# A sliding-window copy on three DMA rings: another order of the rings' DMAs, one release of SyncE's list, 24 merged pairs

## The chip, the cores and the metric

The kernel runs on one core of one Trainium2 chip. The metric is the device time of one execution in microseconds (us), the median of several runs. The core has 16 DMA engines. DMAs are issued by three of its processors here: SyncE (SP), ScalarE (ACT) and GpSimd (POOL). Each has a ring of its own, whose packets all run on the same 16 engines. The profile shows SP's ring as q1, ACT's as q10 and POOL's, which software fills, as q0.

## What is computed

```python
def setup_inputs():
    batch, length, dim = (32, 4096, 256)
    window_size = 64
    stride = 32
    return {'x': np.random.randn(batch, length, dim).astype(np.float32), 'window_size': window_size, 'stride': stride}

def reference(x: np.ndarray, window_size: int, stride: int) -> np.ndarray:
    batch, length, dim = x.shape
    n_windows = (length - window_size) // stride + 1
    result = np.zeros((batch, n_windows, window_size, dim), dtype=np.float32)
    for i in range(n_windows):
        start = i * stride
        result[:, i] = x[:, start:start + window_size].copy()
    return result
```

It is a pure copy. A batch of x has 4096 rows of 1 KB. In blocks of 32 rows (32 KB) it has 128 blocks, and window w of its 127 windows is block w followed by block w + 1. So the output is 127 x 64 KB for each of 32 batches, 266 MB, and nearly every block is written twice: as the first half (half 0) of one window and as the second half (half 1) of the window before.

## The kernel before

No engine computes. The 32 batches are copied in two ways.

**Staged batches.** Twelve batches (the list `staged`, L151) go through the on-chip memory. `Staging.load` (L78) brings a batch into one of six tiles of 128 partitions by 32 KB, a block a partition: one DMA of 4 MB, or four of 1 MB for the first batch. `Staging.store` (L93) then writes all 128 blocks twice, once for each half, in one DMA of 4 MB or two of 2 MB a half. All of these are issued by ACT, in the order that `run` (L121) gives: six loads, six batches' stores, six loads, four batches' stores, and last `store_pair` (L102) for the last two batches. A load waits until the tile's former stores have landed, and a store until its load has. Since 128 blocks are written for 127 windows, each half's store also writes one block too many, into the batch beside it: half 0 of the next batch's window 0, or half 1 of the last window (126) of the batch before. `store_pair` first issues four stores, counted by the semaphore `spilt`, and one more, then waits for `spilt`, then issues the last three.

**Direct batches.** The other twenty (`direct`) are copied from x to the output in memory, by `Copier.windows` (L29): a DMA of n rows, each a half window (32 KB, when `half` is given) or a whole window (64 KB). Two rings share each direct batch but the last:

- SP's ring (`ring_d`) copies half windows, 16 rows (512 KB) a DMA, `blocks` (L166), from the list `halves` (L174): for each batch, windows 0, 16, 32, 63, 79, 95 and 111 as first window, and for each of them half 0 and then half 1. Pieces that a neighbour's staged store overwrites (`spoilt`, L175) are taken out and copied at the end of the list, each behind a wait for that neighbour's stores (L198 to L201). All of SP's DMAs add to `done`.
- POOL's ring (`ring_r`) copies windows 48 to 62, which SP leaves out, 15 whole windows (960 KB) a DMA, `remainder` (L170). `piece` is the longest run in elements: `DIRECT` lets a packet be 32 KB, `DIRECT // 2` halves it to 16 KB. The last batch's windows 48 to 62 come in parts, one DMA of 11 rows and four of 2 half rows, placed between the others (L183 to L187).

All engines read their instructions in order, so a wait holds back everything behind it on that engine. POOL issues its 24 DMAs without waiting. SP issues one DMA, waits until the software ring's DMA for `direct[7]` (`back[7]`) has landed, issues two, waits for `back[11]`, issues three, waits for `back[16]`, and then issues all the rest (L191 to L197), as fast as its ring takes them. The last thing on SP is a wait for every semaphore's total (L203).

Of the kernel before, what the change touches and what calls it, by code (L numbers as in the profile page):

```python
# [8 lines left out]
DIRECT, IN, OUT = 32768, 16384, 16384  # L9
# [124 lines left out]
@with_exitstack  # L134
def kernel(
    ctx: ExitStack,
    tc: tile.TileContext,
    x: bass.AP,
    window_size: bass.AP,
    stride: bass.AP,  # L140
    out: bass.AP,
):
    nc = tc.nc
    W, S = int(window_size), int(stride)
    B, L, D = x.shape
    n_win = (L - W) // S + 1
    assert out.shape == (B, n_win, W, D)
    c = Copier(x, out, B, L, D, W, S, n_win)


    staged = [1, 4, 7, 10, 13, 16, 19, 22, 24, 26, B - 3, B - 2]  # L151
    place = {b: g for g, b in enumerate(staged)}
    direct = [b for b in range(B) if b not in staged]
    pool = ctx.enter_context(tc.tile_pool(name="xb", bufs=1))
    st = Staging(c, tc, pool, x.dtype, staged, 6)
    ring_d, ring_s, ring_r = nc.sync, nc.scalar, nc.gpsimd
    done = tc.alloc_semaphore("done")
    rest = tc.alloc_semaphore("rest")
    back = {i: tc.alloc_semaphore(f"back{i}") for i in (7, 11, 16)}
    total = {done: 0, rest: 0, **dict.fromkeys(back.values(), 0)}  # L160

    def count(dma, sem):
        dma.then_inc(sem, 16)
        total[sem] += 16

    def blocks(part):  # L166
        for b, w, half in part:
            count(c.windows(ring_d, b, w, 16, half), done)

    def remainder(b, w, n, half=None, piece=DIRECT, sem=rest):  # L170
        count(c.windows(ring_r, b, w, n, half, piece), sem)

    first, last = 48, B - 1
    halves = [(b, w + (15 if w >= first else 0), half) for b in direct for w in range(0, 112, 16) for half in (0, 1)]  # L174
    spoilt = {(b + d, 0 if d > 0 else c.nw - 16, 0 if d > 0 else 1): g for b, g in place.items() for d in (1, -1) if b + d in direct}  # L175
    halves = [h for h in halves if h not in spoilt]
    spoilt = sorted(spoilt, key=spoilt.get)
    with tc.tile_critical():
        st.run(ring_s)

        pairs = iter([(first + d, half) for d in (0, 2) for half in (0, 1)])
        for i, b in enumerate(direct[:-1]):
            if i in (8, 9, 12, 13):  # L183
                w, half = next(pairs)
                remainder(last, w, 2, half, DIRECT // 2)
            if i == 3:
                remainder(last, first + 4, 11)  # L187
            remainder(b, first, 15, piece=DIRECT // 2 if i in (1, 2, 3, 13, 15, 18) else DIRECT, sem=back.get(i, rest))
        ring_r.drain()  # L189

        blocks(halves[:1])  # L191
        ring_d.wait_ge(back[7], 16)
        blocks(halves[1:3])
        ring_d.wait_ge(back[11], 16)
        blocks(halves[3:6])
        ring_d.wait_ge(back[16], 16)
        blocks(halves[6:])  # L197
        for h in spoilt:  # L198
            b = h[0] + (-1 if h[1] == 0 else 1)
            st.wait_stored(ring_d, place[b])  # L200
            blocks([h])  # L201
        total[st.ended] = st.count[st.ended]
        for sem, n in total.items():  # L203
            ring_d.wait_ge(sem, n)
# [35 lines left out]
```

## Time and profile before

| what | value |
|---|---|
| median of 3 runs | 748.66 us (748.11 to 748.69) |
| the profiled execution | 747.83 us |
| its span, first to last instruction | 746.1 us |
| bytes moved by DMA | 317.50 MB |
| read from memory, written to memory | 216.79 MB, 267.12 MB |
| SP's DMAs | 280 of 512 KB, median 84.0 us from issue to landing |
| ACT's DMAs | 15 loads, 38 stores |
| POOL's DMAs | 24 (19 of 960 KB, 1 of 704 KB, 4 of 64 KB) |
| busy time of POOL, the only engine that shows any | 13.9 us |

The span runs from the first instruction to the last. A DMA packet is one run of bytes on one DMA engine, data or the 4 bytes that count a semaphore; "from issue to landing" contains the time that a DMA stands in its ring. The DMA share is the mean busy share of the 16 engines in a slice or a window, and is up to a few per cent over 1 where a packet reaches into the next window. An SP or ACT instruction that issues a DMA also lasts as long as its ring is full.

### The profile page before, as it was taken

To read this page: it belongs to the slowest core of one execution; us is meant where nothing else is said; L and a number is where in the kernel's file an instruction comes from. 1 tells how busy PE (TensorE), PEld (TensorE's weight loads), DVE (VectorE), ACT (ScalarE), POOL (GpSimd) and SP (SyncE) were. 2 spreads that over 40 slices of the span, in tenths; PEclk is the share of its full clock that TensorE was granted. 3 is DMA by queue.
4 is the path that set the end of the run, shared out by engine and by line. 5 is a ranking of instruction groups with operands and counts; after the bars stand their busy time and mean duration, and the time that the engine had idled before them with its cause. 6 is when DMAs were issued, how large, how long until landed. Compare 5 with 4: busy or idle time off the path is not lost. (4 is left out here: it accounts for less than half of the span.)

```text
span 746.1 us, 414 instructions
## 1 busy us (share of the span) xinstructions
POOL 13.9 (2%) x28
## 2 busy tenths in 40 slices
POOL 7000000000000000000000000000000000000000
DMA  8999999999999999999999999999999999999998
GB/s 358 437 420 420 430 418 423 428 430 434 429 430 434 429 430 431 433 430 433 432 401 432 431 433 435 428 428 437 429 429 436 430 430 433 430 428 435 429 430 350
DMA packets 20370, 317.50 MB, mean 426 GB/s; under 512 B 5884, under 2 KB 5884, under 8 KB 5884
## 3 DMA queue, kind: packets, MB, share of 16 engines
q10 hardware_dynamic: 10064, 151.00, 47.6%
q1 hardware_dynamic: 8960, 146.82, 46.1%
q0 software_dynamic: 1344, 19.66, 6.2%
q14 instruction: 2, 0.02, 0.0%
HBM read 216.79 MB, written 267.12 MB: 649 GB/s over the span
## 5 line engine op out<-in xcount | busy, mean ns | idle before, releaser
L34 POOL DMA_DIRECT2D out_dram<-in_x_dram x24 | 13.7, 576 | 1.1 <-PEq L235 1.1
L221 POOL MEMSET const-float32-0.0<- 128x1 f32 x1 | 0.1, 98 | 0.2 <-issue 0.2
L221 POOL MEMSET const-bfloat16-1.0<- 128x1 bf16 x1 | 0.1, 101 | 0.0
L221 POOL MEMSET const-float32-1.0<- 128x1 f32 x1 | 0.1, 98 | 0.0
L221 POOL MEMSET const-uint8-127<- 128x1 uint8 x1 | 0.1, 98 | 0.0
## 6 DMA issues: line engine op xcount, KB each, us to landing
out_dram<-in_x_dram SPq DMA_DIRECT2D x280, 512.0 KB, 84.0
out_dram<-xb ACTq DMA_DIRECT2D x28, 2048.0 KB, 105.9
xb<-in_x_dram ACTq DMA_DIRECT2D x11, 4096.0 KB, 121.1
out_dram<-xb ACTq DMA_DIRECT2D x10, 4096.0 KB, 120.2
out_dram<-in_x_dram POOLq DMA_DIRECT2D x19, 960.0 KB, 51.7
xb<-in_x_dram ACTq DMA_DIRECT2D x4, 1024.0 KB, 15.3
out_dram<-in_x_dram POOLq DMA_DIRECT2D x1, 704.0 KB, 21.5
out_dram<-in_x_dram POOLq DMA_DIRECT2D x4, 64.0 KB, 54.1
```

The source lines that it names most:

```text
L34: return q.dma_start(out=self.oap((b * self.nw + w0) * 2 + h, [[2 * blk, n], row]), in_=self.xap(b * self.nb + w0 + h, [[blk, n], row]), m ...
L221: nc = _bacc.Bacc("TRN2", target_bir_lowering=False, num_devices=1)
```

## The change

Four things change, and the bytes copied do not.

- POOL's order: the four 2-row DMAs stand before indices 8, 9, 11 and 14 (before: 8, 9, 12, 13), the one of 11 rows before index 4 (before: 3), and the DMAs cut to 16 KB packets are 1, 3, 4, 6 and 15 (before: 1, 2, 3, 13, 15, 18).
- SP's waits: instead of three, there is one, behind the first DMA, for the last 15-row DMA of the software ring (index 18, the last of that ring). Everything else of SP's follows it.
- Merged pairs: for the 17 direct batches but the first two and the last, half 0 of windows 79 to 94 and 95 to 110 becomes one DMA of 32 rows (1 MB); for seven of them (b % 5 is 0 or 2) half 1 does too. SP then has 256 DMAs.
- Batches by halves: within a batch, `halves` has all of half 0 and then all of half 1.

```diff
-    back = {i: tc.alloc_semaphore(f"back{i}") for i in (7, 11, 16)}
-    total = {done: 0, rest: 0, **dict.fromkeys(back.values(), 0)}
+    back = tc.alloc_semaphore("back")
+    total = {done: 0, rest: 0, back: 0}
...
     def blocks(part):
-        for b, w, half in part:
-            count(c.windows(ring_d, b, w, 16, half), done)
-
-    def remainder(b, w, n, half=None, piece=DIRECT, sem=rest):
-        count(c.windows(ring_r, b, w, n, half, piece), sem)
+        for b, w, half, *n in part:
+            count(c.windows(ring_d, b, w, *(n or [16]), half), done)
+
+    def remainder(i, b, w, n, half=None, piece=DIRECT):
+        count(c.windows(ring_r, b, w, n, half, piece), back if i == len(direct) - 2 and n == 15 else rest)
 
     first, last = 48, B - 1
-    halves = [(b, w + (15 if w >= first else 0), half) for b in direct for w in range(0, 112, 16) for half in (0, 1)]
+    halves = [(b, w + (15 if w >= first else 0), half) for b in direct for half in (0, 1) for w in range(0, 112, 16)]
...
+    for b in direct[2:-1]:
+        halves[halves.index((b, 79, 0))] = (b, 79, 0, 32)
+        halves.remove((b, 95, 0))
+        if b % 5 in (0, 2):
+            halves[halves.index((b, 79, 1))] = (b, 79, 1, 32)
+            halves.remove((b, 95, 1))
...
-            if i in (8, 9, 12, 13):
+            if i in (8, 9, 11, 14):
                 w, half = next(pairs)
-                remainder(last, w, 2, half, DIRECT // 2)
-            if i == 3:
-                remainder(last, first + 4, 11)
-            remainder(b, first, 15, piece=DIRECT // 2 if i in (1, 2, 3, 13, 15, 18) else DIRECT, sem=back.get(i, rest))
+                remainder(i, last, w, 2, half, DIRECT // 2)
+            if i == 4:
+                remainder(i, last, first + 4, 11)
+            remainder(i, b, first, 15, piece=DIRECT // 2 if i in (1, 3, 4, 6, 15) else DIRECT)
         ring_r.drain()
 
         blocks(halves[:1])
-        ring_d.wait_ge(back[7], 16)
-        blocks(halves[1:3])
-        ring_d.wait_ge(back[11], 16)
-        blocks(halves[3:6])
-        ring_d.wait_ge(back[16], 16)
-        blocks(halves[6:])
+        ring_d.wait_ge(back, 16)
+        blocks(halves[1:])
```

## The prediction

> **What bounds the kernel now.** I read the page's parts 2 and 3 first: no compute engine works, so the only question is how busy the DMA engines are and how fast they move bytes while busy.
>
> ```profile
> DMA  8999999999999999999999999999999999999998
> GB/s 358 437 420 420 430 418 423 428 430 434 429 430 434 429 430 431 433 430 433 432 401 432 431 433 435 428 428 437 429 429 436 430 430 433 430 428 435 429 430 350
> DMA packets 20370, 317.50 MB, mean 426 GB/s; under 512 B 5884, under 2 KB 5884, under 8 KB 5884
> ...
> q10 hardware_dynamic: 10064, 151.00, 47.6%
> q1 hardware_dynamic: 8960, 146.82, 46.1%
> q0 software_dynamic: 1344, 19.66, 6.2%
> ```
>
> The 16 engines are busy from end to end: nothing on the chip waits for an idle DMA engine except at the two ends. q10 is ACT's ring (loads and stores of staged batches), q1 SP's ring (the direct copies), q0 POOL's software ring. Time can change only through bytes (317.50 MB, which the change leaves alone), through the rate, and at the ends. Next, the windows view, cut where the rate changes; its columns are window, length, POOL, clock, DMA share and GB/s.
>
> ```profile
> 0.00:10.00 10.00, 8.69 (x19) 1.00 0.77 300
> 10.00:45.00 35.00, 5.25 (x10) 1.00 1.01 430
> 45.00:98.00 53.00, 0.00 (x0) 1.00 1.00 424
> 98.00:120.00 22.00, 0.00 (x0) 1.00 1.00 413
> 120.00:365.00 245.00, 0.00 (x0) 1.00 1.01 431
> 365.00:390.00 25.00, 0.00 (x0) 1.00 1.00 410
> 390.00:702.00 312.00, 0.00 (x0) 1.00 1.01 431
> 702.00:740.00 38.00, 0.00 (x0) 1.00 1.01 430
> 740.00:746.00 6.00, 0.00 (x0) 1.00 0.43 183
> ```
>
> The steady rate is 431 GB/s, and it is reached whenever nothing disturbs. So the span is 317.50 MB / 431 GB/s = 736.7 us, plus what each window loses against 431: the start 10 x (431-300)/431 = 3.0; 10 to 98, 0.1 + 0.9 = 1.0; 98 to 120, 0.9; 365 to 390, 1.2; the end 0.1 + 3.5 = 3.6. Sum 746.4, against a span of 746.1. That execution took 747.83 (1.7 around the span), the median is 748.66, 0.83 more; I carry the difference that I find over to the median.
>
> Third, how the rings share an engine: the DMA view, for 120 to 365 and then for 45 to 98.
>
> ```profile
> q1 hardware_dynamic: 3368, 55.19, 52.5%
> q10 hardware_dynamic: 3368, 50.46, 48.1%
> ```
> ```profile
> q10 hardware_dynamic: 666, 10.34, 46.4%
> q0 software_dynamic: 670, 9.50, 42.1%
> q1 hardware_dynamic: 160, 2.62, 11.8%
> ```
>
> The packet counts of two rings that are both full are equal, 3368 to 3368 and 666 to 670: an engine takes one packet from each ring in turn, whatever its size. A packet may be 32 KB (1213 ns in the trace's packet records), 16 KB (611 ns) or the 4 bytes that count a semaphore (9 ns). A 16-row DMA of SP is, per engine, one 32 KB packet and one of 4 bytes, so two turns, and ACT moves 16 KB in each.
>
> Last, what SP and ACT wait for.
>
> ```profile
> SPq L34 <- DMA out_dram<-in_x_dram: 94.3, 3, 44.5
> SPq L34 <- DMA out_dram<-xb: 44.4, 2, 40.6
> SPq L204 <- DMA out_dram<-xb: 39.7, 1, 39.7
> ```
> ```profile
> 0.91 7.16 ACTq L43 DMA_DIRECT2D xb<-in_x_dram  x9
> ```
>
> SP's three waits for the software ring end at 46, 69 and 98.9 us in the trace. They cost nothing: ACT has queued nine loads (25 MB) by 8 us and POOL all 24 DMAs by 15 us, and the windows show the engines full meanwhile. The 40.6 us is SP's wait for the spilt stores before its last two DMAs; SP's ring holds about 17 DMAs then, which cover it.
>
> **The change, part by part.**
>
> *Merged pairs.* 24 DMAs go, 16 semaphore packets each: 384 packets, 24 an engine, by 9 ns = 0.2 us. Nothing hides it, since the engines are full; bounds 0 and 0.2, I take -0.2. Issue gets cheaper too, but SP issues behind a full ring and gains nothing. The merges also move turns: each takes one turn of SP's away in which ACT moved 16 KB, so SP's list gets ahead of ACT's by 24 turns.
>
> *Release by the last 15-row DMA.* Before, the software ring's last DMA lands at 110.7 us and SP has landed 8 DMAs by then. After, SP has 1. The software ring no longer shares with 7 x 0.524 = 3.7 MB, worth 8.7 us at 424 GB/s; one fewer of its DMAs is cut into 16 KB pieces (5, not 6), so 30 packets fewer, 2 turns an engine, in which ACT moves 0.5 MB or 1.2 us. It should land its last at about 110.7 - 8.7 - 1.2 = 101 us, and SP's list goes then, not at 98.9. SP's waiting is covered as before: ACT's first loads last to 132 us. Behind the wait stand all of SP's other DMAs, and nothing waits for those but the end. ACT, one packet for each of the software ring's, is where it was; SP is 7 DMAs, 14 turns, behind.
>
> *The two together at the end.* SP gains 24 turns and loses 14: its list ends 10 turns sooner against ACT's. Before, the rings ended within 1 us (743.3 and 744.2), SP last by about a turn. After, ACT has some 9 turns left alone: 9 x 16 engines x 16 KB = 2.4 MB, 5.5 us of the same work in another order. No window shows ACT alone. Bounds: at 431 GB/s it costs 0; at the 300 GB/s of the first 10 us, whose ramp makes it too dark, 2.4/0.300 - 5.5 = +2.5. I take 0, nearer the row of two rings with 16 KB packets (430 in 10 to 45). The spilt stores still end under SP's backlog, which shrinks from 17 DMAs by about 10 turns, 5 DMAs, to 12, so SP's last two again cost nothing.
>
> *Software ring's order, batches by halves.* Same bytes, no wait. Where a DMA of 15, 11 or 2 rows puts its rows, the page doesn't show. If each starts on the engine behind the last one's, the four pairs start on engines 3, 4, 3, 4 before and 3, 4, 4, 3 after: no engine's load changes; if not, an engine gets one 32 KB packet more or less, 1.2 us either way at most. I take 0. What can change is who touches memory near whom, and with it the slow stretches: 0.9 in 45 to 98, 0.9 in 98 to 120 (SP in batch 0), 1.2 in 365 to 390 (SP in batch 14 with w from 16 to 63, ACT ending batch 16's stores). The trace shows no cause for them. Bounds: all gone, -3.1; twice as much, +3.1. SP's five early DMAs no longer run as a third ring, and the windows with SP among three are slower (424, 413) than the two-ring one (430): I take a tenth of the whole, -0.3.
>
> In 100 to 120 the rate stays low after the software ring is empty (415 before 110, 413 after). The Trainium skill, HBM Reference, Specifications, gives some 716 GB/s for the memory that a pair of cores shares; three full rings would ask for up to 431 x 1.8 = 776 GB/s, read and written, and by that rule the 12 us of three rings go at 398, so that taking them apart gains 0.9. The row at 413 with two rings speaks against it as the cause; by the rule the sum would be 0.6 lower, still no measurable change.
>
> Sum: -0.2 + 0 + 0 - 0.3 = -0.5: 747.3 for the profiled execution, **748.2 us** for the median.
>
> **The rivals.**
>
> *A, the slow stretches dissolve (faster).* SP's new order puts batch 0 and batch 14 against other work of ACT's. For it: outside these stretches 600 us go at 431. Against: two of the three lie where SP or POOL merely copies as everywhere, so new meetings are as likely as old ones. Two thirds gone: -2.1 - 0.2 = 746.4.
>
> *B, the order by halves brings new slow stretches (slower).* Before, consecutive DMAs of SP write both halves of a window; after, seven or so in a row write the same half, 32 KB at a step of 64 KB, beside ACT's stores, which do the same. For it: the worst row (410) is one of SP copying beside ACT's stores of one half. Against: ACT's stores have this form for most of the run, at 431. One such stretch costs 0.9 to 1.2; it decides from two more on: 748.2 + 2.1 = 750.3, three give 751.3. Call it 750.7.
>
> *C, a ring alone is slow (slower).* ACT's 5.5 us alone at 300 GB/s: 748.2 + 2.5 = 750.7. From 1.7 dearer, some 330 GB/s, it shows. If the merges did not shift turns, SP would be left alone instead, with 14 turns, 7 DMAs or 3.7 MB, at the end; at 300 GB/s +3.7, 751.9. Against: equal packet counts in three windows.
>
> *D, the merge saves each DMA's fixed time.* SP's DMAs land one in 2.4 us while taking 84 us from issue to landing, so latency is hidden; if 2.4 us were a price by DMA and not by byte, 24 x 2.4 = 58 us would go: 690. The full engines exclude nearly all of it.
>
> **How the numbers follow.** About 0.2% (1.5 us) is what a measurement of this kernel can tell from no change. Forecast 0.50; A 0.26; B 0.15; C 0.08; D 0.01. Faster than 747.2: A and D, 0.27. Slower than 750.2: B and C, 0.23. The forecast's own range is 747.2 to 749.6; taking in the greater part of A and of B and C, 746.1 to 751.0.
>
> **What would show it.** Right: SP has one long wait that ends near 101 us; q1 has 8576 packets; the steady windows still give 431; SP's last data lands some 5 us before ACT's, and the last windows hold their rate. A shows as 45 to 120 and the stretch near batch 14 at 429 or more; B as windows under 425 after 120 us that were at 431; C as a low rate in the last 6 us before the end. I am wrong if SP ends last, if its wait ends far from 101, or if the time is outside the forecast's range with all windows at 431.

## The result and the profile after

The changed kernel took 751.07 us (median of 6 runs, 750.39 to 752.89), the kernel before 748.67 on the same chip (6 runs, 747.51 to 749.06): a ratio of 1.0035, interval 1.0025 to 1.0045. It is slower by 2.4 us, where 748.2 and no change was forecast. The profiled execution took 751.22, its span is 749.4, which is 3.3 more than before.

The page of the changed kernel, parts 2 and 3:

```profile
DMA  8999999999999999999999999999999999999998
GB/s 359 428 432 428 431 433 433 427 433 425 432 432 421 433 433 426 429 433 428 407 431 414 431 427 422 424 429 433 422 428 432 429 420 428 425 429 431 417 431 344
DMA packets 19954, 317.49 MB, mean 424 GB/s; under 512 B 5498, under 2 KB 5498, under 8 KB 5498
...
q10 hardware_dynamic: 10064, 151.00, 47.5%
q1 hardware_dynamic: 8576, 146.82, 46.1%
q0 software_dynamic: 1312, 19.66, 6.1%
```

The engines are as full as before and move the same bytes, with q1 down to the expected 8576 packets. What differs is the rate, from the tenth slice on: 421, 426, 414, 422 where the kernel before held about 430. The windows (start and end, length, POOL, clock, DMA share, GB/s), cut as in the prediction:

```profile
0.00:10.00 10.00, 8.70 (x19) 1.00 0.78 300
10.00:45.00 35.00, 5.25 (x10) 1.00 1.01 428
45.00:98.00 53.00, 0.00 (x0) 1.00 1.01 429
98.00:120.00 22.00, 0.00 (x0) 1.00 1.02 433
120.00:365.00 245.00, 0.00 (x0) 1.00 1.01 429
365.00:390.00 25.00, 0.00 (x0) 1.00 1.00 411
390.00:702.00 312.00, 0.00 (x0) 1.00 1.01 427
702.00:740.00 38.00, 0.00 (x0) 1.00 1.01 423
740.00:749.00 9.00, 0.00 (x0) 1.00 0.64 273
```

The same account as before: 317.49 MB / 431 GB/s = 736.6 us, plus the loss of each window: start 3.0; 10 to 120, 0.2 + 0.2 - 0.1 = 0.3 (before 1.9); 120 to 365, 1.1 (before 0); 365 to 390, 1.2 (1.2); 390 to 702, 2.9 (0); 702 to the end, 0.7 + 3.3 = 4.0 (3.6). Sum 749.1, against 749.4. So the change did win 1.6 us in the first 120, where the release and POOL's order act (no run has one without the other), and the steady part, which cost nothing before, gives 4.0 away.

SP's waits and, from 120 to 365, the turns:

```profile
SPq L34 <- DMA out_dram<-in_x_dram: 97.1, 1, 97.1
SPq L34 <- DMA out_dram<-xb: 51.4, 3, 41.1
```
```profile
q1 hardware_dynamic: 3283, 55.78, 53.3%
q10 hardware_dynamic: 3291, 49.43, 47.3%
```

One wait of SP's for the software ring is left and ends at 98.7 us in the trace, a little ahead of the 101 forecast. The rings still take turns packet by packet, 3283 to 3291, merges or not: with fewer 4-byte packets SP moves 55.78 MB in that window to ACT's 49.43, where it was 55.19 to 50.46.

In the trace's packet records the slow time is in data packets that last longer than their 611 ns (16 KB) or 1213 ns (32 KB). What they last beyond that, their surplus, sums to 3.8 us an engine over the steady part (130 to 350 and 410 to 695 us), where the kernel before has 0.4.

### The profile page after: what moved, and what is told of

Its sections match the earlier page's. It is cut to its first block, busy times and chain, and to the rows that moved or that the text cites. A ratio compares the mean times of both kernels' runs of the same rounds, so it can differ in the third digit from the quotient of the medians.

```text
span 749.4 us, 389 instructions
## 1 busy us (share of the span) xinstructions
POOL 13.9 (2%) x28
## 2 busy tenths in 40 slices
DMA packets 19954, 317.49 MB, mean 424 GB/s; under 512 B 5498, under 2 KB 5498, under 8 KB 5498
## 3 DMA queue, kind: packets, MB, share of 16 engines
q1 hardware_dynamic: 8576, 146.82, 46.1%
```

## The experiments

Each group of kernels ran on a chip of its own, with the kernel before timed beside it. That took 745.4 to 745.6 us on the first four groups' chips and 748.2 on the last one's; 748.7 had been measured at first. So only times of one group are compared.

**First group: each part taken out.** Three kernels undo or isolate a part; the fourth keeps the merges but deals the rows out in another way.

```diff
# no merge: the changed kernel without these lines
-    for b in direct[2:-1]:
-        halves[halves.index((b, 79, 0))] = (b, 79, 0, 32)
...
# merge alone: the kernel before with those lines and blocks() taking n
# no halves: the changed kernel
-    ... for b in direct for half in (0, 1) for w in range(0, 112, 16)]
+    ... for b in direct for w in range(0, 112, 16) for half in (0, 1)]
# rows apart: the changed kernel, for n == 32
+                out=self.oap((b * self.nw + w0) * 2 + h, [[2 * blk, 16], [32 * blk, 2], row]),
+                in_=self.xap(b * self.nb + w0 + h, [[blk, 16], [16 * blk, 2], row]),
```

> The changed kernel with all of SP's DMAs at 16 rows again (280 of them); the order by halves, the single release and POOL's order stay. Theory M (the merged DMAs stretch the packets around them): the windows from 120 to 700 us return to 431 GB/s outside batch 14, and the time is 748 to 749 if SP alone at the end is fast. SP lacks 14 turns without the merges, so it is left alone with some 7 DMAs (3.7 MB, about 8 us); if a ring of copies alone is slow this adds 1 to 4 us to the end and nowhere else. Theory H (the order by halves does it): windows from 200 to 700 stay at 427 to 428, time 751.

> The kernel before with the 24 merged pairs and nothing else. Theory M: 427 to 428 GB/s over 200 to 700 us, 751 us or more. Theory H: 431, 748.5. In both SP's list ends 24 turns ahead of ACT's, so ACT's stores are alone for the last 13 to 15 us; if a lone ring of stores is as fast as two, the last windows stay at 430.

> The changed kernel with each batch in the old order (window, then half); merges, single release and POOL's order stay. Theory M: still 750.5 to 751.5. Theory H: 748 to 748.7, windows at 431.

> The changed kernel, but a merged DMA's 32 rows are walked so that each DMA engine gets rows e and e + 16 (as two 16-row DMAs would give it) in place of rows 2e and 2e + 1. The number of packets and turns is that of the changed kernel. If merging harms by the wider step between the engines' addresses (128 KB in the output), the time is 748 to 749. If it harms because an engine takes two 32 KB copies of SP to one semaphore packet, or for a reason outside the merges, it is 751 as it was.

| kernel | us | before | ratio (interval) |
|---|---|---|---|
| no merge | 748.78 | 745.40 | 1.0045 (1.0030 to 1.0060) |
| merge alone | 746.42 | 745.40 | 1.0013 (1.0003 to 1.0022) |
| no halves | 746.29 | 745.40 | 1.0011 (1.0002 to 1.0020) |
| rows apart | 745.67 | 745.40 | 1.0005 (0.9996 to 1.0015) |

None of the four shows the loss of the steady part: all hold 431 or 432 GB/s from 120 to 350 and from 410 to 695. The one that is clearly dearer is the kernel without merges (the others are at most 1.0 us over the kernel before), and its loss stands elsewhere. Its windows, first with both rings, then with SP's copies alone, and the DMA view from 728 to 740 us:

```profile
715.00:726.00 11.00, 0.00 (x0) 1.00 1.05 445
728.00:738.00 10.00, 0.00 (x0) 1.00 1.00 347
```
```profile
q1 hardware_dynamic: 252, 4.13, 99.8%
q10 hardware_dynamic: 1, 0.00, 0.0%
```

The first window goes at the full rate (its 445 counts packets that reach beyond it, share 1.05). ACT's ring is empty from 728 on; SP's copies have the engines for themselves, keep them busy (share 1.00) and still move only 347 GB/s. A 32 KB packet that lasts 1213 ns beside ACT's stores lasts about 1475 here. From 727 to 745 us the same view has 5.64 MB of SP's, which is what it was left with: 5.6/0.347 - 5.6/0.431 = 3.1 us, nearly all of the 3.4 lost. That is what the merges are good for here: they bring SP's list forward so that it doesn't end alone.

A copy reads and writes memory, so 347 GB/s are 694 GB/s of memory traffic. The Trainium skill, HBM Reference, Specifications, gives about 716 GB/s for the memory of a pair of cores: this trace agrees, with 694 just under it, and so it does with the page's remark that a lone core streams at about what its 16 DMA engines carry (431 here). That the memory is what holds the copies is argued: an engine that lost time between two copies in a row would look the same, and no run separates the two.

The opposite end is seen with merges alone, where SP's list ends 12 us before ACT's:

```profile
731.00:737.00 6.00, 0.00 (x0) 1.00 1.01 431
737.00:743.00 6.00, 0.00 (x0) 1.00 0.61 262
```

ACT's stores alone run at 431: a ring of stores loses nothing. The last 6 us only show that the engines don't stop together.

**Second group: the changed kernel on another chip**, since the first group had met no loss to explain. Halves alone is the kernel before with the new order of the list (the line shown above) and nothing else.

> The changed kernel itself, on the chip of this call, as the measure for the others. In the first four runs the steady windows went at 431 GB/s with merges and without, in either order of the halves, so neither theory alone is left: either it takes both, the order by halves and merged rows that lie side by side (theory HM), or the slow packets of the changed kernel belonged to the chip it was profiled on (theory chip). HM: 2 to 3 us over the kernel before, windows 200 to 700 at 427 to 428. Chip: within 1 us of the kernel before and of the kernel with rows apart, windows at 431.

> The kernel before with each batch by halves and nothing else. HM and chip: no dearer than before by more than 1 us, windows 200 to 700 at 431. If the order by halves harmed alone: +2 or more.

> The changed kernel with rows e and e + 16 on an engine, on the same chip as the changed kernel. HM: about 2 us less than the changed kernel, level with before. Chip: level with the changed kernel.

> The changed kernel in the old order of halves, merges kept, on the same chip as the changed kernel. HM: 1.5 to 2.5 us less than the changed kernel. Chip: level with it.

| kernel | us | before | ratio (interval) |
|---|---|---|---|
| changed | 745.55 | 745.52 | 0.9999 (0.9990 to 1.0008) |
| halves alone | 745.53 | 745.52 | 1.0001 (0.9992 to 1.0010) |
| rows apart | 745.37 | 745.52 | 0.9999 (0.9991 to 1.0008) |
| no halves | 745.80 | 745.52 | 1.0004 (0.9996 to 1.0013) |

All level. The changed kernel costs nothing on this chip, as theory "chip" has it. Theory HM, by which merges and order by halves together must cost 2 to 3 us, loses its ground here.

**Third group: again, and what the slow stretches hang on.**

```diff
+    turn = [b for b in direct if b not in (0, 14)]
+    turn[turn.index(20):turn.index(20)] = [14]
+    turn[-1:-1] = [0]
+    halves.sort(key=lambda h: turn.index(h[0]))
```

> The changed kernel once more, to see whether the 2.4 us that it cost at first go with the chip. If the kernel before is near 745.5 on this chip, the changed one should be within 0.7 us of it; if it is near 748.7, theory chip says 2 to 3 us over it, with the windows of 200 to 700 us at 427 to 428.

> Rows e and e + 16 on an engine, on the same chip. On a chip where the changed kernel loses 2 us or more: level with the kernel before if the loss is the meeting of half order and side-by-side rows, level with the changed kernel if not. On a chip where it loses nothing: level with both.

> The kernel before with each batch by halves. On a chip where the changed kernel loses: as slow as it if the order by halves is enough, level with before if it takes merges too. Else level with before.

> The changed kernel with SP's batch 0 moved behind batch 28 and batch 14 behind batch 18. It tells what the slow stretches hang on. If on the addresses of batches 0 and 14: the windows 98 to 120 and 365 to 390 go at 430, and stretches of 0.5 us loss each come where the two batches now stand (about 440 to 475 for batch 14, 600 to 650 for batch 0). If on the moment (the ring's release at 98 us, ACT's change from stores to loads near 370 us): both stay where they were.

Before took 745.56; changed 745.49 (1.0001, 0.9991 to 1.0010), rows apart 745.56 (0.9999), halves alone 745.81 (1.0005), batches moved 745.57 (1.0003, 0.9993 to 1.0013): level. The last one answers a question of the prediction. Its windows, where the stretches were and then where batches 14 and 0 now stand:

```profile
112.00:122.00 10.00, 0.00 (x0) 1.00 1.03 419
122.00:360.00 238.00, 0.00 (x0) 1.00 1.00 430
360.00:378.00 18.00, 0.00 (x0) 1.00 1.00 411
```
```profile
431.00:461.00 30.00, 0.00 (x0) 1.00 1.01 431
633.00:663.00 30.00, 0.00 (x0) 1.00 1.00 430
```

The stretches stayed at their moment, and the batches took nothing with them. The later one goes with ACT's change from its first six batches' stores to the next loads: the last of these loads, which waits for the sixth batch's stores, is issued at 377.6 us in the kernel before and at 363.3 in the one without merges, and the stretched packets lie from 372 to 382 and from 361 to 367. What happens in that moment to slow the packets stays open.

**Fourth group: another chip.**

> The changed kernel on whatever chip this call gets. Theory chip: where the kernel before takes about 748.7, the changed one takes 2 to 3 us more and shows packets stretched all over 200 to 650 us; where it takes 745.5, they are level.

> The changed kernel in the old order of halves, merges kept. On a chip where the changed kernel loses: level with before if the order by halves is needed for the loss, as slow as the changed one if the merges are enough. Else level with all.

> The kernel before by halves alone, no merges, early waits. On a chip where the changed kernel loses: as slow as it if the order by halves is enough, level with before if it takes the merges too. Else level with all.

Before 745.46; changed 745.50 (1.0000, 0.9991 to 1.0010), no halves 746.12 (1.0009, 0.9999 to 1.0018), halves alone 745.51 (1.0005, 0.9995 to 1.0014). Level a third time.

**Fifth group: a chip like the first.**

> The changed kernel on the chip of this call. Level with the kernel before if that takes 745.5; 2 to 3 us over it if that takes 748.7.

> The kernel before by halves alone. Where the changed kernel loses: as slow as it if the order by halves is enough, level with before if not. Else level with all.

> The changed kernel with rows e and e + 16 on an engine. Where the changed kernel loses: level with before if the loss is in merged rows that lie side by side, as slow as the changed kernel if not. Else level with all.

| kernel | us | before | ratio (interval) |
|---|---|---|---|
| changed | 751.29 | 748.17 | 1.0046 (1.0031 to 1.0061) |
| halves alone | 749.03 | 748.17 | 1.0014 (1.0004 to 1.0024) |
| rows apart | 751.17 | 748.17 | 1.0043 (1.0027 to 1.0059) |

Here the loss is back, with the kernel before as slow as at first. Windows up to 120 us and of the steady part, for the changed kernel, halves alone and rows apart:

```profile
45.00:120.00 75.00, 0.00 (x0) 1.00 1.01 430
120.00:350.00 230.00, 0.00 (x0) 1.00 1.01 429
410.00:695.00 285.00, 0.00 (x0) 1.00 1.01 426
```
```profile
45.00:120.00 75.00, 0.00 (x0) 1.00 1.01 426
120.00:350.00 230.00, 0.00 (x0) 1.00 1.01 430
410.00:695.00 285.00, 0.00 (x0) 1.00 1.01 430
```
```profile
45.00:120.00 75.00, 0.00 (x0) 1.00 1.01 432
120.00:350.00 230.00, 0.00 (x0) 1.00 1.01 428
410.00:695.00 285.00, 0.00 (x0) 1.00 1.01 426
```

And for comparison the changed kernel on the fourth group's chip:

```profile
120.00:350.00 230.00, 0.00 (x0) 1.00 1.01 431
410.00:695.00 285.00, 0.00 (x0) 1.00 1.01 431
```

Three things follow. The loss belongs to the pair of kernel and chip: the same kernel goes at 431 on one chip and at 426 to 429 on another. (Each of the five groups' chips was used once, so that it is the chip and not the occasion isn't shown.) The order by halves alone takes 0.9 us of it (by its interval 0.3 to 1.8), with the steady part at 430. And the rows' neighbourhood on an engine is not the cause, since rows apart loses the same; that the other walk does change which rows an engine copies is taken from the kernel, as the packet records have no addresses.

What is left are the merges and the early parts of the change (release, POOL's order). The early ones act before 99 us, where the changed kernel is the faster (430 or 432 against 426), but they also leave SP's list 20 turns further behind ACT's for the rest of the run. In the packet records, the 24 merged DMAs and 1 us on either side make up 30% of the steady part's time and hold 2.9 of its 5.0 us of surplus in the changed kernel, 3.3 of 5.3 with rows apart, and 2.3 of 3.8 in the first profile. The kernel with halves alone has 1.1 us in all. So more than half of the surplus lies at the merges, in under a third of the time. The 1.5 to 2.1 us outside them are also more than halves alone has, and what makes those stays open.

Not shown is whether the merges stretch packets in the old order of halves too: merges without the new order weren't run on such a chip, nor was the release alone.

## Why the prediction was wrong

**The bound and the account** held: bytes over 431 GB/s plus the losses of the windows gives the span of both kernels within 0.3 us.

**The merged pairs** are the step that failed, as far as the runs show. They were costed at -0.2 and otherwise as turns that only move the end; that the rate stays at 431 beside them was taken without a reason. On two of the five occasions on which the changed kernel ran it fell to 426 to 429 over the steady part, with more than half of the surplus at the merges. Why is argued. A merged DMA gives an engine two 32 KB copies of SP in three turns, to three 16 KB packets of ACT; two 16-row DMAs give two to four. The copies' share rises from 64 of 128 KB to 64 of 112, and with it the memory traffic that full engines ask for, counting a copy twice: 431 x 96/64 = 646 GB/s for single DMAs, 431 x 176/112 = 677 for merged ones. The prediction had the packet sizes for that sum and didn't make it. Copies alone moved 694 in a later run, so 677 leaves little; that some chips slow there already and others don't fits the numbers, but isn't measured.

**The release**: that SP would go at about 101 us came out at 98.7, and the three-ring stretch was worth more than the 0.3 taken: 1.6 us over 10 to 120 on the first chip, together with POOL's order. The row that spoke against it, 413 after the software ring was empty, decides nothing. On the first chip that slow stretch went with the change (98 to 120 at 433); on a faster one there was a slow stretch with the rings apart (112 to 122 at 419 with batches moved). The estimate from the Trainium skill's figure (HBM Reference, Specifications), by which taking the rings apart gains 0.9, came nearer to the 1.6 than the 0.3 that was taken.

**The two together at the end**: the signs were right, the size wrong. By the packet records SP is 71 packets an engine behind ACT from 110 us on in the kernel before and 91 to 92 in the changed one. So the release cost 20 turns, not 14. About 13 are those that were forecast. The others are a delay that the sum left out: SP's wait ends at 98.7 us, its first packet comes at 102.5, and in between ACT has the engines alone. From 98.4 to 102.4 us the windows and the DMA view have:

```profile
98.40:102.40 4.00, 0.00 (x0) 1.00 1.01 434
```
```profile
q10 hardware_dynamic: 120, 1.74, 101.4%
```

That costs no time, as the engines stay full, but it is 7 to 8 turns of ACT's. Before, SP ended last by about 1 us; with 24 turns gained and 20 lost ACT is alone for 1.3 us at the end (last data 746.4 and 747.7), not 5.5. Without merges SP is left with 5.6 MB, some 11 DMAs or 21 turns, which agrees. Had it been 5.5, it would still have cost nothing, as taken: stores alone run at 431.

**The slow stretches** were placed by SP's batches 0 and 14, with no cause seen; on a faster chip they keep their moment when the batches are moved. The term itself, -0.3, had the wrong sign on the first chip: 3.1 us over 10 to 702 became 5.5, by the account above.

**The rivals.** A (stretches dissolve) did not come. B (the order by halves brings new ones) had the size, 750.7, and the place, windows after 120 us (at 427 to 429, not under 425), but its mechanism alone carries 0.9 of 3.1 us in the last group. C had its second branch right: SP alone at the end is slow, 347 GB/s, and the kernel without merges pays 3.4 us for it where 3.7 was said; in the changed kernel it doesn't arise. D was excluded: with 24 DMAs fewer the changed kernel is level at best, where 58 us were to go.

On three chips the forecast of no change holds to 0.1%, in part by luck, since small terms cancel there. Beside halves alone on the same chips, the changed kernel has 0.3 to 0.7 us less surplus from 10 to 98 us, but 0.3 to 0.5 more from 350 to 410 and 0.1 to 0.8 more over the steady part. The prediction had one chip's windows and no term for how such a chip takes another mix.

## What to carry to other kernels

When all DMA engines are full, cost an edit by the turns that it moves between rings, by the turns that pass between a wait's end and the first packet behind it, and by the memory traffic of the mix, with a copy from memory to memory counted twice, and let the ring of stores, not the ring of copies, end last. A 0.3% verdict on a kernel whose DMA engines are full may belong to the chip: run the kernel on a second one before taking the change up or throwing it out.

## What was not expected of the hardware

Copies from memory to memory alone move 347 GB/s with all engines busy, 694 read and written, while stores alone or half and half with copies reach 431. An engine takes one packet from each full ring in turn, and a 4-byte semaphore packet takes a turn like a 32 KB one (3368 to 3368 packets, 3283 to 3291 after). A ring whose list was held back gets its first packet 3.8 us after its wait ends. And chips, or occasions, differ: the kernel before took 745.5 us on four chips and 748.2 to 748.7 on two occasions more, with a granted clock of 1.0 throughout.
